# A two-layer recurrent decoder step: the last layer norm taken apart, and the variance products of the others moved

## The chip, the cores and the metric

The kernel runs on one core of a Trainium2 chip. A core has a matrix engine (TensorE, PE in the profile), a vector engine (VectorE, DVE), an engine for activation functions (ScalarE, ACT), a general one (GpSimd, POOL) and a synchronisation engine (SyncE, SP), each with its own instruction queue, and 16 DMA engines. The metric is device time in microseconds. The time before is 1552.72 us, the median of three runs (1552.39 to 1553.37).

## The reference

One step of a decoder trunk with two layers (width 1024), over a prompt of 512 tokens and 8 samples of 4 tokens. Layer 0 mixes by mLSTM and gated linear attention, layer 1 by a Mamba-2 state space mixer (SSD); each is followed by a squared-ReLU MLP. After each of the four blocks stands a layer norm over the features:

```python
def _layernorm(x, g, b):
    xf = x.astype(jnp.float32)
    mu = xf.mean(-1, keepdims=True)
    var = jnp.square(xf - mu).mean(-1, keepdims=True)
    y = (xf - mu) * lax.rsqrt(var + LN_EPS) * g.astype(jnp.float32) + b.astype(jnp.float32)
    return y.astype(x.dtype)

def _mlp(x, w1, w2):
    return jnp.square(jax.nn.relu(x @ w1)) @ w2
...
x = LN(DN_ALPHA * x + mix(x))
x = LN(DN_ALPHA * x + mlp(x))
```

## The kernel before

**Layout.** The 544 tokens are two halves of 272 columns (`TH`). Activations lie feature-major: a tile is 128 features by 272 tokens, and `KT` = 8 tiles make the width. `xf[hf]` holds the eight float32 tiles of a half, `xh` and `xl` their high and low parts for the matrix engine. A float32 product is made of three fast ones, high by high, high by low, low by high. `dense` (L359) issues them for one output tile and half: 24 for eight tiles of contraction, into one of three PSUM buffers (`psd`), and then the eviction, VectorE's add of `psd` to `xf` (L390, L392). I call one product of `dense` a dense product.

**Weights.** SyncE loads a weight block into `wraw` (three buffers), ScalarE makes its high part `whi` (L166), VectorE the low part `wlo` (L167), 1024 columns at a time.

**Order.** TensorE's order is written out by hand. Beside the dense products run lanes, Python generators that issue other TensorE work: `tick()` advances them ahead of each dense product, and a generator that yields the number N is left alone for N dense products. The table `W` holds these numbers. The order on VectorE, ScalarE, GpSimd and SyncE is made by a scheduler from a timeline that it simulates for the whole program. So a change of one place also moves instructions of these four engines elsewhere.

**The norms.** The last `phase` of a block runs tile 0 of both halves, then tiles 1 to 7 of half 0, then 1 to 7 of half 1 (`TAIL` = 7; behind the first mixer it is all eight). `residual` evicts a tile and adds it to the half's running sum `lns`, on GpSimd for tiles 1 to 6 (L396, L398) and on VectorE for tile 7. After a half's last tile `layernorm` is launched as a lane:

- the mean product L411, a matmul with a matrix of ones, which sums over the 128 features of `lns`
- four operations of two tiles each that take the mean off (VectorE, L416), and their squares `lnq` (ScalarE, L417)
- four adds that bring the eight squares down to one tile (GpSimd L419, VectorE L420 to L422)
- after `v0` = 60 (half 0) or `v1` = 55 (half 1) dense products the variance product L426
- logarithm and exponential for the inverse root (ScalarE, L428, L429)
- eight scalings (VectorE, L432), and the high, low and full parts for the next block (L439 to L441).

There are four norms: behind the first mixer, behind the first MLP (`mlp`), behind the SSD mixer (`ssd_out`) and behind the second MLP, which is the last. The last writes its tiles to the output (L434, and a transfer per pair). For its half 1 nothing dense is left: it leaves tile 7 out of the running sum (`short`), adds it by a second mean product (L413), and takes all eight squares as eight variance products (L426) in place of the adds.

**The SSD mixer.** In its first group, around 750 us, ScalarE copies convolution inputs `ci` from PSUM (L1351, L1354, L1356), issues small transfers from its queue, among them `dec` (L1317) and `decs` (L1319, two, decay factors of the samples broadcast to 64 partitions) and `ec` (L1408), and takes the activation `Cf` (L1369). VectorE makes the columns `scols` and `ncs` (L1335, L1336). The diff doesn't touch these lines.

## Time and profile before

| what | value |
|---|---|
| median of three runs | 1552.72 us |
| the profiled execution's own time | 1552.4 us |
| its span | 1550.5 us |
| TensorE busy | 1490.8 us, 96% |
| VectorE busy | 1086.5 us, 70% |
| ScalarE busy | 794.7 us, 51% |
| GpSimd busy | 307.3 us, 20% |
| granted TensorE clock, mean | 0.99 |

The busy time of a matmul is modelled and overlaps with that of the next, so 96% does not mean that TensorE is at its best; its waits are what counts. The span is the time between the first and the last profiled instruction. A row of the waits names who waits and for whom, then the wait in all, how often, and the longest. A row of the timeline has the start, the duration of one instruction or the busy time of several (x8), the engine, the line, the operation, output and input by the program's names, and in square brackets the engine's idle time ahead of it with what ended it. The chain has start, duration, engine and line of the work that ended last, in order of time. In a row of the windows stand the window, its length, then busy time and instructions of an engine.

### The profile page before, as it was taken

What the parts mean: (1) busy time and instruction counts of PE and PEld (TensorE: products, weight loads), DVE (VectorE), ACT (ScalarE), POOL (GpSimd) and SP (SyncE); (2) the same over time, 40 slices, a digit from 0 to 9 for tenths busy, and PEclk for the clock granted to TensorE, in tenths of its full rate; (3) what the DMA queues carried; (4) which work ended last, traced back from release to release, by engine and by line L of the source; (5) the groups of instructions that cost most, each with busy time, mean ns of one, the idle gap of its engine ahead of it and who ended that gap; (6) DMA issues with size and microseconds to landing.
All of it is one profiled execution on the core that took longest, in us unless ns stands there. A gap on an engine that the chain in (4) does not pass through costs nothing.

```text
span 1550.5 us, 29292 instructions
## 1 busy us (share of the span) xinstructions
PE 1490.8 (96%) x11621; PEld 1436.3 (93%) x11621; DVE 1086.5 (70%) x2029; ACT 794.7 (51%) x1749; POOL 307.3 (20%) x369
## 2 busy tenths in 40 slices
PE   8899999999999999999899999999899999999997
PEld 7799988999999999999797789989899999999996
DVE  4963466686776677658799978667768767676644
ACT  5543455474444444537685766645238344344333
POOL 0420223310000000043253464533330000000011
PEclk9999999999999999999999999999999999999999
DMA  6221222513333233415547768364213333323221
GB/s 217 65 83 55 59 87 69 180 39 97 96 105 94 89 96 85 146 40 198 114 125 248 209 180 261 96 208 136 69 34 87 99 85 105 97 86 95 66 83 58
DMA packets 88400, 172.11 MB, mean 111 GB/s; under 512 B 15464, under 2 KB 41960, under 8 KB 88008
## 3 DMA queue, kind: packets, MB, share of 16 engines
q1 hardware_dynamic: 52296, 141.20, 29.2%
q10 hardware_dynamic: 33376, 18.42, 4.8%
q0 software_dynamic: 2592, 10.62, 1.7%
q8 instruction: 91, 1.49, 0.4%
q14 instruction: 45, 0.37, 0.1%
HBM read 153.48 MB, written 16.73 MB: 110 GB/s over the span
## 4 chain that ended last, share of the span: by engine, by line
PE 79%; DVE 7%; ACT 3%; DMA 2%; issue 2%; ACTq 1%; POOL 0%; DVEq 0%; SPq 0%; POOLq 0%
PE psd L359 53%; PE psd L449 16%; DVE wlo L167 1%; PE num L693 1%; ACT whi L166 1%; PE yp L1472 1%; DMA E<-d_cs 1%; PE it L1519 1%; PE sp L1450 1%; DVE xf L416 1%; DVE h0n L1532 1%; DVE xl L1586 1%; PE var L426 1%; PE ip L1447 1%; ACTq L1319 1%
## 5 line engine op out<-in xcount | busy, mean ns | idle before, releaser
L359 PE MATMUL psd<-xh,whi 128*128 128x272 f32 x1504 | 447.5, 298 | 7.4 <-ACT xh L283 6.0
L359 PE MATMUL psd<-xh,wlo 128*128 128x272 f32 x1504 | 443.6, 295 | 0.2 <-DVE wlo L167 0.2
L359 PE MATMUL psd<-xl,whi 128*128 128x272 f32 x1504 | 442.8, 294 | 0.3 <-DVE xl L284 0.3
L359 PEld LDWEIGHTS psd<-xh,whi 128*128 128x128 f32 x1504 | 287.0, 191 | 14.1 <-ACT xh L283 6.4
L359 PE MATMUL psd<-hh,whi 128*128 128x272 f32 x1024 | 296.6, 290 | 3.6 <-DVE xf L392 2.5
L359 PE MATMUL psd<-hlo,whi 128*128 128x272 f32 x1024 | 295.4, 289 | 0.2
L359 PE MATMUL psd<-hh,wlo 128*128 128x272 f32 x1024 | 295.4, 288 | 0.0
L359 PEld LDWEIGHTS psd<-xl,whi 128*128 128x128 f32 x1504 | 287.0, 191 | 6.6 <-issue 4.0
L359 PEld LDWEIGHTS psd<-xh,wlo 128*128 128x128 f32 x1504 | 286.7, 191 | 4.5 <-issue 3.0
L166 ACT CAST whi<-wraw 128x1024 fp32r<-128x1024 f32 (+2 forms) x173 | 174.4, 1011 | 160.6 <-PE psd L359 138.2
L167 DVE TENSOR_TENSOR wlo<-wraw,whi 128x1024 fp32r<-128x1024 f32 (+2 forms) x173 | 210.2, 1217 | 65.8 <-ACT whi L166 65.1
L359 PEld LDWEIGHTS psd<-hh,whi 128*128 128x128 f32 x1024 | 192.8, 188 | 5.8 <-DVE xf L392 4.4
L359 PEld LDWEIGHTS psd<-hlo,whi 128*128 128x128 f32 x1024 | 192.8, 188 | 0.7 <-DVE hlo L284 0.6
L359 PEld LDWEIGHTS psd<-hh,wlo 128*128 128x128 f32 x1024 | 192.7, 188 | 0.1
L392 DVE TENSOR_TENSOR xf<-xf,psd 128x272 f32<-128x272 f32 x208 | 88.3, 433 | 92.2 <-PE psd L359 91.4
L396 POOL TENSOR_TENSOR lns<-xf 128x272 f32<-128x272 f32 x8 | 9.1, 1138 | 684.1 <-DVE xf L392 678.8
L449 PE MATMUL psd<-xh,whi 128*128 128x272 f32 x416 | 120.2, 289 | 0.9 <-DVE xf L392 0.9
L449 PE MATMUL psd<-xh,wlo 128*128 128x272 f32 x416 | 119.9, 288 | 0.0
L449 PE MATMUL psd<-xl,whi 128*128 128x272 f32 x416 | 119.6, 288 | 0.0
L202 ACT CAST whi<-wsum 128x1024 fp32r<-128x1024 f32 x52 | 54.3, 1044 | 121.4 <-PE psd L449 72.1
L202 ACT CAST whi<-wraw 128x1024 fp32r<-128x1024 f32 (+1 forms) x52 | 43.4, 835 | 96.6 <-PE psd L359 85.3
L203 DVE TENSOR_TENSOR wlo<-wsum,whi 128x1024 fp32r<-128x1024 f32 x52 | 63.7, 1224 | 23.2 <-ACT whi L202 23.2
(448 smaller groups left out, 2962.4 us busy)
## 6 DMA issues: line engine op xcount, KB each, us to landing
wraw<-mlp_w SPq DMA_DIRECT2D x80, 512.0 KB, 3.6
wraw<-ssd_in SPq DMA_DIRECT2D x40, 512.0 KB, 4.3
wraw<-mlp_w SPq DMA_DIRECT2D x64, 256.0 KB, 3.1
wraw<-ab_in SPq DMA_DIRECT2D x24, 512.0 KB, 3.7
h<-h SPq DMA_DIRECT2D x32, 256.0 KB, 4.6
h0n<-h0n SPq DMA_DIRECT2D x16, 512.0 KB, 5.0
E<-d_cs ACTq DMA_DIRECT2D x16, 512.0 KB, 5.1
s_h<-h0n POOLq DMA_DIRECT2D x16, 512.0 KB, 4.0
```

Source lines behind the costliest of these rows:

```text
L166: nc.scalar.copy(hi[:, r], w[:, r])
L167: nc.vector.tensor_tensor(lo[:, r], w[:, r], hi[:, r].bitcast(F32), ALU.subtract)
L202: self.cut[0] = nc.scalar.copy(hi, x).ins
L203: self.cut[1] = nc.vector.tensor_tensor(lo, x, hi.bitcast(F32), ALU.subtract).ins
L359: last[0] = TE.matmul(ps[:, :TH], wt[:, k, :], rt, start=i == 0, stop=i == n - 1).ins
L392: V.tensor_tensor(x, x, ps, ALU.add)
L416: V.scalar_tensor_tensor(x[:, k:k + 2], mu[:, None, :n].broadcast_to([P, 2, n]), -1.0 / D, x[:, k:k + 2], ALU.mult, ALU.add)
L426: TE.matmul(var[:, :n], ones, q[:, k], start=k == 0, stop=k == KT - 1 or not short)
L449: last[0] = TE.matmul(ps, wt[:, k], bt[:, k], start=first and n == 0, stop=n == 11, skip_group_check=not first).ins
L693: TE.matmul(num[i], sT[:, i] if j == i else sT[:, (4, 7, 9)[j] + i - j - 1], vt[key][:, j, h, :w], start=j == 0, stop=j == i)
L1319: S.dma_start(out=decs[64 * e:64 * e + 64], in_=d_dec[None, e::2, 4:].broadcast_to([64, 16, NB]))
L1447: TE.matmul(ip[:, j * P:(j + 1) * P], hT[:, j * P:(j + 1) * P], Cf[:, tk], start=True, stop=True)
```

## The change

The variance product of `layernorm` moves from 60 to 76 dense products behind the start of its wait in half 0, and from 55 to 62 in half 1. Half 1 of the last norm gets a function of its own, `last_layernorm`, launched at the eviction of tile 5:

- after `f0` = 10 dense products the mean product of the sum of six tiles (tiles 0 to 5); this mean m6 is taken off all eight tiles, the tiles that aren't finished included, and the first six are squared and added up
- after `f1` = 30 more the variance product of these squares; then, for tile 6 and for tile 7 when each is evicted, a mean product and a variance product of that tile
- the mean that is left over is that of tiles 6 and 7 (the first six now sum to nought), and the variance is the mean of squares less its square (L480, L481)
- logarithm and exponential, the left-over mean taken off in four operations, and `normed`, the scalings and transfers as before.

`short` falls away. The diff:

```diff
-W = dict(..., l0=12, l1=12, v0=60, v1=55)
+W = dict(..., l0=12, l1=12, v0=76, v1=62, f0=10, f1=30)
...
-    def residual(first, ln=None, short=False):
+    def residual(first, ln=None, last_norm=None):
...
             if ln is not None:
-                if m == 1:
+                if hf and last_norm is not None and m >= KT - 2:
+                    ready.add(("last", m))
+                elif m == 1:
                     sums[hf] = ln.tile([P, TH], F32, tag="lns", name="lns", bufs=2)
                     G.tensor_tensor(sums[hf], xf[hf][:, 0], x, ALU.add)
-                elif m > 1 and not (short and hf and m == KT - 1):
+                elif m > 1:
                     (V if m == KT - 1 else G).tensor_tensor(sums[hf], sums[hf], x, ALU.add)
+                if hf and last_norm is not None and m == KT - 3:
+                    launch(last_norm(), "last")
...
-        short = out is not None and hf == 1
-        TE.matmul(mu[:, :n], ones, sums[hf], start=True, stop=not short)
-        if short:
-            TE.matmul(mu[:, :n], ones, x[:, KT - 1], start=False, stop=True)
+        TE.matmul(mu[:, :n], ones, sums[hf], start=True, stop=True)
...
-        for k in range(KT if short else 1):
-            TE.matmul(var[:, :n], ones, q[:, k], start=k == 0, stop=k == KT - 1 or not short)
+        TE.matmul(var[:, :n], ones, q[:, 0], start=True, stop=True)
...
+        if out is not None:
+            normed(x, g, b, rs, out[hf])
+            return
...
+    def last_layernorm(i, pool, out):
+        g, b = lnp[:, 16 * i:16 * i + 8], lnp[:, 16 * i + 8:16 * i + 16]
+        n, x = TH, xf[1]
+
+        def less(mu, k, f):
+            V.scalar_tensor_tensor(x[:, k:k + 2], mu[:, None, :n].broadcast_to([P, 2, n]), f, x[:, k:k + 2], ALU.mult, ALU.add)
+        yield W["f0"]
+        mu = pm("mu")
+        TE.matmul(mu[:, :n], ones, sums[1], start=True, stop=True)
+        q = pool.tile([P, KT, n], F32, tag="lnq", name="lnq", bufs=1)
+        less(mu, 6, -1.0 / (6 * P))
+        for k in (0, 2, 4):
+            less(mu, k, -1.0 / (6 * P))
+            S.activation(q[:, k:k + 2], x[:, k:k + 2], AF.Square)
+        V.tensor_tensor(q[:, 0:2], q[:, 0:2], q[:, 2:4], ALU.add)
+        V.tensor_tensor(q[:, 0:2], q[:, 0:2], q[:, 4:6], ALU.add)
+        V.tensor_tensor(q[:, 0], q[:, 0], q[:, 1], ALU.add)
+        yield W["f1"]
+        yield from need(("last", KT - 2))
+        mu, var = pm("mu"), pm("var")
+        TE.matmul(var[:, :n], ones, q[:, 0], start=True, stop=False)
+        for k in (6, 7):
+            yield from need(("last", k))
+            TE.matmul(mu[:, :n], ones, x[:, k], start=k == 6, stop=k == 7)
+            S.activation(q[:, k], x[:, k], AF.Square)
+            TE.matmul(var[:, :n], ones, q[:, k], start=False, stop=k == 7)
+        ms, v = q[:, 0], q[:, 1]
+        with tc.high_priority():
+            S.activation(ms, mu[:, :n], AF.Square, scale=1.0 / D)
+            V.scalar_tensor_tensor(v, var[:, :n], 1.0 / D, ms, ALU.mult, ALU.subtract)
+        rs = pool.tile([P, n], F32, tag="lnr", name="lnr", bufs=2)
+        S.activation(rs, v, AF.Ln, bias=epsc)
+        S.activation(rs, rs, AF.Exp, scale=-0.5)
+        for k in range(0, KT, 2):
+            less(mu, k, -1.0 / D)
+        normed(x, g, b, rs, out[1])
...
-                phase(8, hrhs(m), n, residual(False, xp, out is not None), tail=TAIL,
-                      after=lambda hf: launch(layernorm(hf, 2 * l + 1, xp, out)))
+                end = None if out is None else lambda: last_layernorm(2 * l + 1, xp, out)
+                phase(8, hrhs(m), n, residual(False, xp, end), tail=TAIL,
+                      after=lambda hf: launch(layernorm(hf, 2 * l + 1, xp, out)) if end is None or hf == 0 else None)
```

Lines of the new program are numbered anew: the evictions are L391 and L393, the running sum L399 and L401, the norm's mean product L415, its subtraction L418, its variance product stays L426, scalings are L435 (L443 in `normed`), low parts L437, and the SSD lines stand 47 later (`decs` L1366, `Cf` L1416).

What stands in the engines' queues now is shown at three places. The first is the end of the program. On TensorE, before, the last dense products of tile 7 of half 1 and what follows them:

```order
L359 MATMUL psd<-hh,wlo 128x272
L411 MATMUL mu<-lns,ones 128x272
L413 MATMUL mu<-xf_12707,ones 128x272
L426 MATMUL var<-lnq,ones 128x272 x8
L1865 UNCONDITIONAL_BRANCH
```

Now the mean product of six tiles (L460) stands 31 dense products ahead of the first of these rows:

```order
L472 MATMUL var<-lnq,ones 128x272
L475 MATMUL mu<-xf_12707,ones 128x272
L477 MATMUL var<-lnq,ones 128x272
L359 MATMUL psd<-hh,wlo 128x272
L359 MATMUL psd<-hh,whi 128x272
L359 MATMUL psd<-hlo,whi 128x272
L359 MATMUL psd<-hh,wlo 128x272
L359 MATMUL psd<-hh,whi 128x272
L359 MATMUL psd<-hlo,whi 128x272
L359 MATMUL psd<-hh,wlo 128x272
L475 MATMUL mu<-xf_12707,ones 128x272
L477 MATMUL var<-lnq,ones 128x272
```

Seven dense products stand between the products of tile 6 and those of tile 7, and two small products behind the last dense one where ten stood before.

On VectorE at the same place, before, from the last add of half 0's squares on (`xf_12702` is half 0 of `xf`, `xf_12707` half 1):

```order
L422 TENSOR_TENSOR lnq<-lnq 128x272
L392 TENSOR_TENSOR xf_12707<-xf_12707,psd 128x272
L432 SCALAR_TENSOR_TENSOR xf_12702<-xf_12702,lnp,lnr 128x272 x8
L392 TENSOR_TENSOR xf_12707<-xf_12707,psd 128x272 x4
L416 SCALAR_TENSOR_TENSOR xf_12707<-mu,xf_12707 128x544 x4
L432 SCALAR_TENSOR_TENSOR xf_12707<-xf_12707,lnp,lnr 128x272 x8
```

And now, from half 0's scalings on:

```order
L443 SCALAR_TENSOR_TENSOR xf_12702<-xf_12702,lnp,lnr 128x272 x8
L393 TENSOR_TENSOR xf_12707<-xf_12707,psd 128x272
L457 SCALAR_TENSOR_TENSOR xf_12707<-mu,xf_12707 128x544 x4
L393 TENSOR_TENSOR xf_12707<-xf_12707,psd 128x272
L466 TENSOR_TENSOR lnq<-lnq 128x544
L467 TENSOR_TENSOR lnq<-lnq 128x544
L468 TENSOR_TENSOR lnq<-lnq 128x272
L393 TENSOR_TENSOR xf_12707<-xf_12707,psd 128x272
L457 SCALAR_TENSOR_TENSOR xf_12707<-mu,xf_12707 128x544
L481 SCALAR_TENSOR_TENSOR lnq<-var,lnq 128x272
L457 SCALAR_TENSOR_TENSOR xf_12707<-mu,xf_12707 128x544 x3
L443 SCALAR_TENSOR_TENSOR xf_12707<-xf_12707,lnp,lnr 128x272 x8
```

Three evictions of half 1 (tiles 5, 6 and 7) stand behind half 0's scalings, with the subtraction of m6 and the adds of squares between them; four stood there before, with nothing between.

The second place is the norm behind the SSD mixer, on VectorE, from half 0's scalings to half 1's subtraction. Before:

```order
L432 SCALAR_TENSOR_TENSOR xf_12702<-xf_12702,lnp,lnr 128x272 x8
L440 SCALAR_TENSOR_TENSOR xl_75<-xf_12702,lnp,xh_73 128x272 x2
L392 TENSOR_TENSOR xf_12707<-xf_12707,psd 128x272
L440 SCALAR_TENSOR_TENSOR xl_75<-xf_12702,lnp,xh_73 128x272 x6
L392 TENSOR_TENSOR xf_12707<-xf_12707,psd 128x272
L167 TENSOR_TENSOR wlo<-wraw,whi 128x1024
L392 TENSOR_TENSOR xf_12707<-xf_12707,psd 128x272
L167 TENSOR_TENSOR wlo<-wraw,whi 128x1024
L392 TENSOR_TENSOR xf_12707<-xf_12707,psd 128x272
L398 TENSOR_TENSOR lns<-lns,xf_12707 128x272
L167 TENSOR_TENSOR wlo<-wraw,whi 128x1024
L416 SCALAR_TENSOR_TENSOR xf_12707<-mu,xf_12707 128x544 x4
```

Now, from the low parts on:

```order
L437 SCALAR_TENSOR_TENSOR xl_75<-xf_12702,lnp,xh_73 128x272 x4
L393 TENSOR_TENSOR xf_12707<-xf_12707,psd 128x272
L437 SCALAR_TENSOR_TENSOR xl_75<-xf_12702,lnp,xh_73 128x272
L167 TENSOR_TENSOR wlo<-wraw,whi 128x1024
L437 SCALAR_TENSOR_TENSOR xl_75<-xf_12702,lnp,xh_73 128x272 x3
L393 TENSOR_TENSOR xf_12707<-xf_12707,psd 128x272
L167 TENSOR_TENSOR wlo<-wraw,whi 128x1024
L393 TENSOR_TENSOR xf_12707<-xf_12707,psd 128x272
L167 TENSOR_TENSOR wlo<-wraw,whi 128x1024
L401 TENSOR_TENSOR lns<-lns,xf_12707 128x272
L167 TENSOR_TENSOR wlo<-wraw,whi 128x1024
L418 SCALAR_TENSOR_TENSOR xf_12707<-mu,xf_12707 128x544 x4
```

Between half 0's scalings and the last add to `lns` there were two weight differences (L167), and there are three now.

The third place is ScalarE in the first group of the SSD mixer, around 750 us. Before:

```order
L166 CAST whi<-wraw 128x1024
L1408 DMA ec<-d_ecs 64x4x128
L1354 COPY ci<-psd 128x240
L1356 COPY ci<-psd 128x8x4
L1351 COPY ci<-psd 128x272
L1317 DMA dec<-d_dec 128x32x4
L1319 DMA decs<-d_dec 64x16x8 x2
L1369 ACTIVATE Cf<-acc 128x512
L1370 ACTIVATE Cf<-acc 128x32
```

Now:

```order
L1455 DMA ec<-d_ecs 64x4x128 x2
L1411 ACTIVATE acc<-ci,sprm 128x568
L1455 DMA ec<-d_ecs 64x4x128
L1450 DMA E_9382<-d_cs 32x8x32
L1364 DMA dec<-d_dec 128x32x4
L1398 COPY ci<-psd 128x272
L1366 DMA decs<-d_dec 64x16x8 x2
L1401 COPY ci<-psd 128x240
L166 CAST whi<-wraw 128x1024
L1403 COPY ci<-psd 128x8x4
L1416 ACTIVATE Cf<-acc 128x512
```

The transfers `dec` and `decs` stand behind more transfers than before (`ec`, `E`), and between `decs` and `Cf` there are now a copy, a weight cast and another copy.

More of the change, by code (lines that the diff above doesn't have):

```diff
@@ L33 @@
 HEADM = 6
-W = dict(dec=12, gates=400, sc=16, lev=12, v=8, kd=10, out=33, end=12, c0=15, u=11, s=16, ml=12, dt=238, sg=72, sx=14, sq=26, so=48, l0=12, l1=12, v0=60, v1=55)
+W = dict(dec=12, gates=400, sc=16, lev=12, v=8, kd=10, out=33, end=12, c0=15, u=11, s=16, ml=12, dt=238, sg=72, sx=14, sq=26, so=48, l0=12, l1=12, v0=76, v1=62, f0=10, f1=30)
 LEVELS = (64, 32, 16, 8, 4, 2, 1)
@@ L417, in layernorm @@
             S.activation(q[:, k:k + 2], x[:, k:k + 2], AF.Square)
-        if not short:
-            G.tensor_tensor(q[:, 0:2], q[:, 0:2], q[:, 2:4], ALU.add)
-            V.tensor_tensor(q[:, 4:6], q[:, 4:6], q[:, 6:8], ALU.add)
-            V.tensor_tensor(q[:, 0:2], q[:, 0:2], q[:, 4:6], ALU.add)
-            V.tensor_tensor(q[:, 0], q[:, 0], q[:, 1], ALU.add)
-            yield W["v1" if hf else "v0"]
+        G.tensor_tensor(q[:, 0:2], q[:, 0:2], q[:, 2:4], ALU.add)
+        V.tensor_tensor(q[:, 4:6], q[:, 4:6], q[:, 6:8], ALU.add)
+        V.tensor_tensor(q[:, 0:2], q[:, 0:2], q[:, 4:6], ALU.add)
+        V.tensor_tensor(q[:, 0], q[:, 0], q[:, 1], ALU.add)
+        yield W["v1" if hf else "v0"]
         var = pm("var")
-        for k in range(KT if short else 1):
-            TE.matmul(var[:, :n], ones, q[:, k], start=k == 0, stop=k == KT - 1 or not short)
+        TE.matmul(var[:, :n], ones, q[:, 0], start=True, stop=True)
         rs = pool.tile([P, n], F32, tag="lnr", name="lnr", bufs=2)
@@ L432, in layernorm @@
             V.scalar_tensor_tensor(xk, xk, gk, rs, ALU.mult, ALU.mult)
-            if out is not None:
-                S.activation(xk, xk, AF.Identity, bias=bk)
-                if k % 2 or k == KT - 2:
-                    k0 = k if k >= KT - 2 else k - 1
-                    nc.sync.dma_start(out=out[hf][:, k0:k + 1], in_=x[:, k0:k + 1])
-                continue
             S.activation(xh[hf][:, k], xk, AF.Identity, bias=bk)
@@ L441, in layernorm, with normed @@
             S.activation(xk, xk, AF.Identity, bias=bk)
+    def normed(x, g, b, rs, out):
+        for k in range(KT):
+            xk = x[:, k]
+            V.scalar_tensor_tensor(xk, xk, g[:, k:k + 1], rs, ALU.mult, ALU.mult)
+            S.activation(xk, xk, AF.Identity, bias=b[:, k:k + 1])
+            if k % 2 or k == KT - 2:
+                k0 = k if k >= KT - 2 else k - 1
+                nc.sync.dma_start(out=out[:, k0:k + 1], in_=x[:, k0:k + 1])
+    def last_layernorm(i, pool, out):
[12 more added lines that the diff above has]
+        V.tensor_tensor(q[:, 0:2], q[:, 0:2], q[:, 2:4], ALU.add)
+        V.tensor_tensor(q[:, 0:2], q[:, 0:2], q[:, 4:6], ALU.add)
+        V.tensor_tensor(q[:, 0], q[:, 0], q[:, 1], ALU.add)
+        yield W["f1"]
[17 more added lines that the diff above has]
+        normed(x, g, b, rs, out[1])
     def quarter(w, b, ps, first):
```

## The prediction

> **What bounds the kernel now.** I read the page first, then TensorE's waits, over the whole span and in the windows of the norms, then the chain at the end, then the timelines of the places that the change touches.
>
> ```profile
> span 1550.5 us, 29292 instructions
> ...
> DVE  4963466686776677658799978667768767676644
> ...
> PE 79%; DVE 7%; ACT 3%; DMA 2%; issue 2%; ACTq 1%; POOL 0%; DVEq 0%; SPq 0%; POOLq 0%
> ```
>
> TensorE carries 79% of the chain that ends last. So the time falls only where TensorE waits, and in the stretch behind its last product; work that only moves on another engine costs nothing until TensorE waits for it. VectorE's row has three slices of 38.8 us at 9 (the 21st to 23rd, 775 to 891 us, in the SSD mixer): there a delay on VectorE isn't made up. TensorE's waits that bear on the change:
>
> ```profile
> PE xt L1411 <- DVE ncs L1336: 6.4, 1, 6.4
> ...
> PE var L426 <- ACT lnq L417: 1.6, 1, 1.6
> ```
>
> In the windows 300 to 310, 676 to 690, 1145 to 1155 and 1164 to 1176 us the variance product's wait reads, in turn:
>
> ```profile
> PE var L426 <- DVE lnq L422: 1.5, 1, 1.5
> ...
> PE var L426 <- DVE lnq L422: 0.5, 1, 0.5
> ...
> PE var L426 <- DVE lnq L422: 1.6, 1, 1.6
> ...
> PE var L426 <- DVE lnq L422: 0.6, 1, 0.6
> ```
>
> The columns are the wait in all, how often, the longest. I call the three norms A (behind the first mixer), B (behind the first MLP) and C (behind the SSD mixer). Half 0 of A, B and C waits 1.5, 0.5 and 1.6 us, half 1 of C 0.6: **4.2 us** is all that moving the variance products can win. The 1.6 us of `ACT lnq` is in the end chain, which the new last norm replaces:
>
> ```profile
> 1535.54 0.45 DVE xf L392
> ...
> 1536.87 0.73 DVE xf L416
> 1537.63 0.67 ACT lnq L417
> 1538.34 3.95 PE var L426 x16
> 1542.31 0.49 ACT lnr L428
> ...
> 1543.29 0.51 DVE xf L432
> ```
>
> From the eviction of the last tile to the first scaling is 1543.29 - 1535.54 = 7.75 us, 3.95 of it the eight variance products, 0.49 each.
>
> **The change, part by part.** (1) *Variance products later.* How far one dense product moves another is read from a window at the end:
>
> ```profile
> 1524.00:1534.00 10.00, 10.00 (x82) 10.00 (x81) 1.00 0.31 113
> ```
>
> It counts 82 products, some two of which began before it: 10 / 80 = 0.125 us each. 16 products later is 2.0 us, more than the 1.6 of any half 0; 7 later is 0.88, more than the 0.6. So each of the four waits goes, and I ask at each what is late next. B: nothing (VectorE's slice there reads 5), -0.5. A: ScalarE's new order has a weight cast between the norm's logarithm and its exponential, and that cast waited for its weights:
>
> ```profile
> 310.69 1.05 ACT L166 CAST whi<-wraw 128x1024 fp32r<-128x1024 f32 x1 [1.88 <-DMA wraw<-mlp_w]
> ...
> 324.15 0.62 PE L411 MATMUL mu<-lns,ones 128*128 128x272 f32 x2
> ```
>
> The scalings of half 0 then start late, and the sums of half 1, due at the second row, with them. The cost lies between nothing, if the 12 us from the cast's end make it up, and the whole 1.88 + 1.05; I take 0.3, since those 12 us hold mostly VectorE work that can close up. A gives -1.2. C: VectorE has no gap between the scalings of half 0 and the mean product of half 1:
>
> ```profile
> 1156.29 3.08 DVE L440 SCALAR_TENSOR_TENSOR xl<-xf,lnp,xh 128x272 fp32r<-128x272 f32 x6
> 1159.64 1.21 DVE L167 TENSOR_TENSOR wlo<-wraw,whi 128x1024 fp32r<-128x1024 f32 x1
> 1163.25 0.44 DVE L398 TENSOR_TENSOR lns<-lns,xf 128x272 f32<-128x272 f32 x1
> ...
> 1164.01 0.62 PE L411 MATMUL mu<-lns,ones 128*128 128x272 f32 x2
> ```
>
> The new order puts three weight differences of 1.2 us ahead of the last sum (`lns`) instead of two. So the sum ends no earlier than before, though TensorE gets there 1.6 us sooner, and half 0's 1.6 is given back; half 1's 0.6 stays. Ends: 0 to -1.6 for half 0, and I take 0, because the extra row's 1.21 nearly fills it. **Sum: -1.2 - 0.5 - 0.6 = -2.3**, with ends -4.2 and 0.
>
> (2) *The end chain.* Behind the last eviction the new program needs the mean product (from 1535.54 to 1536.87 before: 1.33 us to the first subtraction), four subtractions, one variance operation of 272 columns and the first scaling. Their rows:
>
> ```profile
> 1514.86 0.62 PE L411 MATMUL mu<-lns,ones 128*128 128x272 f32 x2
> ...
> 1515.53 2.62 DVE L416 SCALAR_TENSOR_TENSOR xf<-mu,xf 128x544 f32<-128x544 f32 x4 [0.98 <-PE mu L411]
> 1516.34 2.49 ACT L417 ACTIVATE lnq<-xf 128x544 f32<-128x544 f32 x4 [23.98 <-DVE xf L416]
> ...
> 1520.39 0.72 DVE L421 TENSOR_TENSOR lnq<-lnq 128x544 f32<-128x544 f32 x1
> ...
> 1524.61 3.39 DVE L432 SCALAR_TENSOR_TENSOR xf<-xf,lnp,lnr 128x272 f32<-128x272 f32 x8 [1.13 <-ACT lnr L429]
> ```
>
> 1.33 + 2.62 + 0.42 (a scaling, 3.39 / 8, the nearest row to the variance operation) = 4.37. Logarithm and exponential (0.49 and 0.46) lie beside the last three subtractions, which cover them. So the first scaling is 7.75 - 4.37 = **3.4 us earlier after the eviction**. What follows it (eight scalings, ScalarE's bias, the transfer) is the same code.
>
> But the eviction itself comes later. Ahead of it are now four fp32 products that weren't (mean and variance of six tiles, mean and variance of the seventh): 4 x 0.49 = 2.0. And two new waits. The mean product L460 stands 38 dense products ahead of the last, so it is due 38 x 0.125 = 4.75 us before the old one:
>
> ```profile
> 1529.51 0.44 DVE L392 TENSOR_TENSOR xf<-xf,psd 128x272 f32<-128x272 f32 x1 [1.16 <-PE psd L359]
> ...
> 1530.10 0.77 POOL L398 TENSOR_TENSOR lns<-lns,xf 128x272 f32<-128x272 f32 x1 [0.83 <-DVE xf L392]
> ...
> 1535.34 0.62 PE L411 MATMUL mu<-lns,ones 128*128 128x272 f32 x2
> ```
>
> That is at 1530.6. It needs the sum of tile 5, whose eviction is the row of 1529.51. Half 0's scalings (3.39 us from 1524.61) are pushed 2.0 us back with their variance product, and in VectorE's order they stand ahead of tile 5's eviction: from 1526.6, or 1526.8 behind tile 4's eviction, to 1530.2, or 1530.7 if GpSimd's add of tile 4 holds one up. So tile 5 is evicted up to 1.2 us late; GpSimd's add starts 0.59 later and takes 0.77: 1531.6 to 1532.1, a wait of 1.0 to 1.5; I take 1.2. Next, the first variance product L472 stands 31 dense products behind, 0.49 + 31 x 0.125 = 4.4 us, and needs 0.67 (mean to subtraction), 2.62, the last square's 0.62, two adds of 0.72 and 0.44, which is 5.1, or 5.5 with an eviction in the way: a wait of 0.7 to 1.1, and I take 1.1, as an eviction does stand there. **Sum: 2.0 + 1.2 + 1.1 - 3.4 = +0.9**; without both waits it is -1.4, with both twice as long +3.2.
>
> The 0.5 is from a pair of rows at C. The first was shown: six operations in 3.08 us, 0.5 more than six of 0.42. The second ran beside them:
>
> ```profile
> 1156.51 0.91 POOL L398 TENSOR_TENSOR lns<-lns,xf 128x272 f32<-128x272 f32 x1 [5.24 <-issue]
> ```
>
> The Trainium skill, page "SBUF — State Buffer", section "Who interferes with whom", has a rule that speaks against this change here: VectorE and GpSimd share one port pair, an exclusive lock, and a VectorE instruction with two SBUF inputs contends with a GpSimd instruction that reads SBUF. These rows agree. By the rule the wait at L460 is 1.5, without it 1.0; the value taken lies between.
>
> (3) *The SSD mixer's first group.* The other engines' order is set by the scheduler's own simulated time, and it comes out differently there, though no line of it is edited. It holds TensorE's longest wait for VectorE, the 6.4 us at 765:
>
> ```profile
> 754.48 0.36 ACT L1354 COPY ci<-psd 128x240 f32<-128x240 f32 x1 [2.89 <-DVE acc L1366]
> ...
> 754.74 0.20 ACT L1356 COPY ci<-psd 128x32 f32<-128x32 f32 x1
> ...
> 755.05 8.13 ACTq L1319 DMA_DIRECT2D decs<-d_dec  x2
> 763.23 0.63 ACT L1369 ACTIVATE Cf<-acc 128x512 f32<-128x512 f32 x1 [8.01 <-issue]
> ...
> 764.60 0.42 DVE L1335 COPY scols<-rt 128x256 f32<-128x256 f32 x1
> ```
>
> ScalarE stands 8.13 us in issuing two transfers (`decs`), and `Cf`, the column copies and TensorE are behind it. In the new order three things that ran ahead of `decs`, or far from it, stand between `decs` and `Cf`: a copy of 0.36, a weight cast of 1.05 (row at 310.69) and a copy of 0.20: +1.6 if `decs` starts and blocks as before. It may start up to 2.9 us earlier (the 2.89 that ScalarE idled), or be blocked longer, since more transfers (`ec`, `E`) are issued ahead of it; half of 8.13 once more is +4, +5.5 with the 1.6. Ends: -6.4 (the wait gone) and +5.5; I take **+1.6**, the one part with rows of its own.
>
> The Trainium skill, page "DMA: Bandwidth & Descriptors", section "Issuing engines are not separate DMA queues", says that the time an engine's sequencer spends starting a DMA is usually small beside the DMA itself. The row of 8.13 us disagrees. By the rule this order would cost nothing and the sum would be 1.6 lower.
>
> **The sum.** -2.3 + 0.9 + 1.6 = +0.2 on the profiled execution's own 1552.4 (1.9 more than its span): **1552.6 us**, no change. The median of the runs, 1552.72, is 0.3 above that execution, within their spread. About 0.2%, 3.1 us, is what a measurement of this kernel can tell from no change.
>
> **The rivals.**
> *Faster.* The weight differences at C fall where VectorE would idle and the sums of the last half are in time: -4.2 and -1.4, with the SSD mixer as it was: 1546.8 us; with (1) as taken, 1548.7. For it: the waits are there in the trace, and every bound of (2) is within 1.5 us of no wait. Against it: VectorE's order at C. Chance 0.25.
> *Slower.* One mechanism, the `decs` issue: if it blocks ScalarE over 2.9 us longer (from where -2.3 + 0.9 + 1.6 + 2.9 = +3.1), TensorE's wait at 765 grows, and VectorE's full slices don't give it back: with +5.5 it is -2.3 + 0.9 + 5.5 = +4.1, 1556.5 us. For it: ScalarE's queue row and the transfers now ahead of it. Against it: the 2.89 of idle time. Chance 0.20.
> *The SSD order costs nothing:* -2.3 + 0.9, 1551.0 us. Chance 0.10. This is the time that the skill's rule on issuing gives.
> *The change doesn't bite:* the variance products wait on, because what makes `lnq` is pushed back by the same evictions: +0.9 + 1.6, 1554.9 us. Against it: 2.0 covers 1.6. Chance 0.07.
> *The forecast* 0.38.
>
> Same: 0.38 + 0.10 + 0.07 = 0.55; faster 0.25; slower 0.20. The range leaves out half of each outer case: 1548 to 1556.5.
>
> **What would show it.** (1): the rows `PE var` for L422's successor are gone; at C the mean product of half 1 is as late behind half 0's variance product as the lost 1.6. (2): from last eviction to first scaling 4.4 us; waits for `lns` and `lnq` of some 1 us each, 5 us before the end. (3): the row `PE xt` near 765 reads about 8. It is wrong if TensorE's waits change in places that I haven't looked at, as in other groups of the SSD mixer, where the order changes little.

## The result, and the profile after

The changed kernel takes 1556.89 us (median of 13 runs, 1554.82 to 1560.26), the kernel before 1551.94 us (13 runs, 1547.12 to 1554.68): 1.0038 times as long, with a 95% interval of 1.0029 to 1.0047. It is slower by 5.0 us in the medians, 5.9 by the ratio. The forecast was 1552.6 us in a range of 1548 to 1556.5.

The page of the changed kernel, its span and the chain's shares by engine:

```profile
span 1555.7 us, 29290 instructions
...
PE 39%; DVE 6%; ACT 3%; issue 2%; DMA 2%; POOL 1%; ACTq 1%; POOLq 0%; DVEq 0%
```

The chain that this page follows back from the end breaks off at 741 us, so its shares add up to about half of the span and can't be set beside the 79% before. TensorE's waits in it (in all, how often, the longest):

```profile
PE xt L1458 <- DVE ncs L1383: 8.5, 1, 8.5
...
PE mu L415 <- DVE lns L401: 3.9, 3, 2.7
...
PE psd L359 <- ACT ci L1403: 1.7, 1, 1.7
...
PE mu L460 <- POOL lns L401: 1.4, 1, 1.4
...
PE var L472 <- DVE lnq L468: 1.1, 1, 1.1
```

The variance products at A, B and C wait no more, 4.2 us before. In their place the **mean products** of half 1 wait for `lns`: 3.9 us in three waits of 0.6, 0.6 and 2.7, which weren't there. The wait of `xt` in the SSD mixer grew from 6.4 to 8.5. The two waits of the new last norm are there as forecast.

Waits alone don't add up to a span, so I matched TensorE's instructions of the two traces in order and took the difference of their starts. One pair of rows, before and after, shows it:

```profile
765.36 0.66 PE L1411 MATMUL xt<-scon,Y 128*128 128x128 f32 x2 [6.39 <-DVE ncs L1336]
```

```profile
767.39 0.45 PE L1458 MATMUL xt<-scon,Y 128*128 128x128 f32 x1 [8.52 <-DVE ncs L1383]
```

There the changed kernel is 2.0 us behind. A part's cost is the difference behind it less that ahead of it, here with bounds at 290, 400, 712, 766, 1130, 1200 and 1515 us of the trace before, and the end of the span. All 17 traces (one of each kernel) are in the table, against the trace before, in us; the experiments follow below. "Ratio" is the timed one, to the kernel before.

| kernel | up to A | A | B | SSD, first group | SSD, rest | C | MLP | tail | ratio (95%) |
|---|---|---|---|---|---|---|---|---|---|
| the changed kernel | -0.3 | -0.5 | 0.3 | **2.5** | 0.4 | **1.6** | -0.4 | **1.6** | 1.0038 (1.0029 to 1.0047) |
| e1_vmove | -1.6 | -0.4 | 0.3 | 2.8 | -0.5 | 1.8 | -0.4 | 0.0 | 1.0030 (1.0017 to 1.0044) |
| e2_lastonly | -0.3 | 0.0 | 0.2 | -0.2 | -0.5 | 0.0 | -0.2 | 0.5 | 1.0011 (0.9997 to 1.0025) |
| e3_C | 2.6 | 0.0 | -0.1 | -0.3 | -0.8 | 0.2 | 0.0 | 0.5 | 1.0021 (1.0011 to 1.0031) |
| e4_AB | -0.1 | -0.6 | 0.1 | 2.7 | 0.3 | 0.0 | -0.3 | 0.4 | 1.0029 (1.0018 to 1.0041) |
| e5_v0 | 2.4 | -0.4 | 0.2 | 0.2 | 2.1 | 1.8 | -0.3 | 1.6 | 1.0016 (1.0002 to 1.0029) |
| e6_v1 | -0.8 | 0.0 | -0.1 | 2.8 | 0.0 | -0.8 | -0.5 | 0.4 | 1.0012 (0.9999 to 1.0026) |
| e7_tail | 0.7 | 0.0 | 0.1 | 0.0 | -3.1 | 0.0 | -0.2 | -0.8 | 0.9998 (0.9982 to 1.0013) |
| e8_decs | -2.0 | -0.5 | 0.1 | -1.8 | -0.1 | 0.2 | -0.4 | 1.7 | 1.0010 (0.9994 to 1.0027) |
| e9_best | -0.6 | -1.5 | -0.4 | 1.6 | -0.6 | 0.0 | -0.3 | -0.7 | 0.9980 (0.9972 to 0.9989) |
| e10_l1 | 5.4 | -0.5 | 0.0 | 2.9 | -2.9 | -2.4 | -0.4 | 1.6 | 1.0018 (1.0008 to 1.0029) |
| e11_v0site | -0.7 | -1.5 | -0.3 | 0.4 | 0.4 | 0.0 | -0.4 | -0.7 | 0.9989 (0.9974 to 1.0004) |
| e12_decs0 | 1.1 | 0.0 | 0.0 | 0.3 | -2.9 | 0.0 | -0.3 | 0.1 | 1.0001 (0.9990 to 1.0012) |
| e13_dec0 | 0.1 | 0.0 | -0.1 | -4.1 | 2.9 | 0.0 | -0.4 | 2.0 | 1.0008 (0.9994 to 1.0022) |
| e14_dec1 | 0.1 | -0.5 | 0.0 | -4.2 | 2.7 | 0.2 | -0.4 | 1.7 | 1.0018 (1.0005 to 1.0031) |
| e15_decbest | 0.6 | -1.5 | -0.4 | -4.3 | 2.8 | 0.0 | -0.4 | -0.7 | 0.9978 (0.9963 to 0.9992) |
| e16_all | -0.8 | -1.5 | -0.4 | -4.3 | 6.7 | -2.4 | -0.3 | -0.7 | 0.9955 (0.9938 to 0.9973) |

The columns "up to A" and "SSD, rest" differ between kernels in which nothing was edited there: they are what one execution differs from another, up to 5 and 7 us. The "MLP" column is the same in nearly all, so it is the trace before that was long there. The other columns repeat to a few tenths of a microsecond wherever the same code runs, with two exceptions that are explained below (C and one tail). On them the verdicts rest, with the timed ratios behind them.

### The profile page after: what moved, and what is told of

Its sections match the earlier page's. It is cut to its first block, busy times and chain, and to the rows that moved or that the text cites. A ratio compares the mean times of both kernels' runs of the same rounds, so it can differ in the third digit from the quotient of the medians.

```text
span 1555.7 us, 29290 instructions
## 1 busy us (share of the span) xinstructions
PE 1490.7 (96%) x11613; PEld 1436.4 (92%) x11613; DVE 1088.7 (70%) x2037; ACT 795.5 (51%) x1751; POOL 306.3 (20%) x368
## 4 chain that ended last, share of the span: by engine, by line
PE 39%; DVE 6%; ACT 3%; issue 2%; DMA 2%; POOL 1%; ACTq 1%; POOLq 0%; DVEq 0%
PE psd L359 26%; PE psd L495 8%; DMA E<-d_cs 1%; DVE wlo L167 1%; ACT E L1479 1%; PE it L1566 1%; PE yp L1519 1%; DVE acc L1413 1%; DVE h0n L1579 1%; DVE xl L1633 1%; PE sps L1573 1%; ACT whi L166 1%; PE sp L1497 1%; DVE xf L393 0%; ACTq L1366 0%
## 5 line engine op out<-in xcount | busy, mean ns | idle before, releaser
L167 DVE TENSOR_TENSOR wlo<-wraw,whi 128x1024 fp32r<-128x1024 f32 (+2 forms) x173 | 208.5, 1207 | 73.0 <-ACT whi L166 69.5
L393 DVE TENSOR_TENSOR xf<-xf,psd 128x272 f32<-128x272 f32 x208 | 88.1, 432 | 94.2 <-PE psd L359 93.7
L399 POOL TENSOR_TENSOR lns<-xf 128x272 f32<-128x272 f32 x8 | 9.1, 1139 | 684.3 <-DVE xf L393 678.9
```

Of the source, the lines that this page charges most:

```text
L167: nc.vector.tensor_tensor(lo[:, r], w[:, r], hi[:, r].bitcast(F32), ALU.subtract)
L393: V.tensor_tensor(x, x, ps, ALU.add)
```

## The experiments: which part costs

Four kernels take the change apart. The first is the kernel before with the numbers alone, the second the changed kernel without them:

```diff
e1_vmove (on the kernel before)
-v0=60, v1=55
+v0=76, v1=62
e2_lastonly (on the changed kernel)
-v0=76, v1=62
+v0=60, v1=55
```

> The kernel before with the two numbers alone moved (v0 76, v1 62), its last norm as it was. Theory (the waits of the variance products were only traded: half 0's scalings and low parts, pushed back by 16 products, now hold up the sum of half 1, and ScalarE's and VectorE's new order in the SSD mixer's first group adds to that): slower by 3 to 5 us, ratio 1.002 to 1.003; no wait of L426 at the three inner norms, but waits of the mean product for lns of some 0.6, 0.6 and 2.7 us, and the wait of xt near 765 some 2 us longer than before. Rival (the loss is the new last norm's, moved variance products win what their waits were): faster by 2 to 4 us, ratio 0.998. Rival (SSD differences are chance from run to run): ratio 1.000.

> The changed kernel with v0 60 and v1 55 as before, so only the new last norm is left of the change; SSD mixer's queues are as before. Theory: half 0's scalings are 2 us earlier than in the changed kernel, so the wait for lns at L460 (1.4 there) is under 0.5; the wait for lnq at L472 stays 1.1; 2.0 of added products + 0.4 + 1.1 - 3.4 = 0.1 us: ratio 0.999 to 1.001. Rival (the loss is in the last norm): slower by 3 us or more, 1.002.

The other two move the products at one place alone, with the new last norm in:

```diff
-        yield W["v1" if hf else "v0"]
+        v0, v1 = (W["v0"], W["v1"]) if i in (2,) else (60, 55)      # e3_C; (0, 1) for e4_AB
+        yield v1 if hf else v0
```

> As the one before, but with the variance products moved (76, 62) at the norm behind the SSD mixer alone; the SSD mixer's queues are as before. Theory: the 1.6 and 0.6 us of waits there go, and a wait for lns of some 2.7 us comes at half 1's mean product: 0.5 to 1.6 us slower than with the new last norm alone. Rival (the moved product is worth its wait): 2 us faster than that.

> As the kernel with the new last norm alone, but with the variance products moved (76, 62) at the first two norms alone; this brings the SSD mixer's other order of ScalarE and VectorE. Theory: norms +0.1 (2.0 of waits gone, as much come back as waits for lns and for the scalings), SSD +2.8: 2 to 3.5 us slower than with the new last norm alone. Rival (the SSD difference is chance): within 0.7 us of it, with the wait of xt near 765 at 6 to 7 us.

Measured: 1.0030, 1.0011, 1.0021 and 1.0029. The loss is in the moved products: they alone make the kernel 4.7 us slower, and the rival that they win what their waits were falls. The last norm alone is not told from no change by the time; its tail is 0.5 us longer in the trace. Both together give 1.0041 against 1.0038 measured. The waits of e1_vmove for `lns` and at `xt`:

```profile
PE xt L1411 <- DVE ncs L1336: 8.8, 1, 8.8
...
PE mu L411 <- DVE lns L398: 3.9, 3, 2.7
```

They come with the numbers alone. Two more kernels tell which of the two numbers brings the SSD mixer's new order: in the first the order of ScalarE and VectorE there is nearly that of before, in the second that of the changed kernel.

```diff
-v0=76, v1=62
+v0=76, v1=55      # e5_v0
+v0=60, v1=62      # e6_v1
```

> The changed kernel with v1 back at 55, so that of the moved variance products only half 0's are left. The SSD mixer's queues are then as before the change. Theory (the SSD mixer's loss comes with v1 alone; half 0's moved products trade their waits for waits for lns): no stall of some 1.9 us at 735, the wait of xt near 765 at 6 to 6.5 us, waits of the mean product for lns of 0.6, 0.6 and 2.7 us; against the new last norm alone between 0 and 1.5 us slower, so ratio 1.001 to 1.002 to the kernel before. Rival (half 0's moved products cost most): 1.003 or more.

> The changed kernel with v0 back at 60, so that only half 1's variance products are moved, by 7, which could win the one wait of 0.6 us. The SSD mixer's queues are those of the changed kernel. Theory: stall of 1.9 us at 735, xt waits 8.5 us, the waits of half 0's variance products (1.5, 0.5, 1.6) are back and those for lns gone; 2 us slower than the new last norm alone, ratio 1.002 to 1.003 to the kernel before. Rival (SSD difference is chance or is made up later): as the new last norm alone, 1.001.

The traces answer as the theory says: first group of SSD 0.2 against 2.8, C 1.8 against -0.8. The times don't settle the split: to e2_lastonly's 1.0011, v0 alone adds 0.0005, v1 alone 0.0001 and both together 0.0027, with intervals of 0.0013 to either side. The time of e6_v1 is even the one that its rival names (1.001), not the 1.002 to 1.003 of its theory. The 2.5 to 2.9 us of the first group stand in all five traces in which v1 is 62 ahead of the SSD mixer and no transfer was moved, and in none of the five with 55 there; how much of it lasts to the end is taken up with the runs on `dec` below.

**Why C gets worse.** VectorE behind the SSD mixer in the changed kernel, from half 0's scalings to half 1's sum, and the scalings before:

```profile
1154.59 3.90 DVE L435 SCALAR_TENSOR_TENSOR xf<-xf,lnp,lnr 128x272 f32<-128x272 f32 x8
...
1161.96 1.84 DVE L437 SCALAR_TENSOR_TENSOR xl<-xf,lnp,xh 128x272 fp32r<-128x272 f32 x3
...
1164.06 1.21 DVE L167 TENSOR_TENSOR wlo<-wraw,whi 128x1024 fp32r<-128x1024 f32 x1
...
1165.55 1.43 DVE L167 TENSOR_TENSOR wlo<-wraw,whi 128x1024 fp32r<-128x1024 f32 x1
1166.90 0.43 DVE L401 TENSOR_TENSOR lns<-lns,xf 128x272 f32<-128x272 f32 x1
```

```profile
1151.81 3.39 DVE L432 SCALAR_TENSOR_TENSOR xf<-xf,lnp,lnr 128x272 f32<-128x272 f32 x8 [1.46 <-ACT lnr L429]
```

The changed kernel is 2.4 us behind when it reaches C. Its scalings begin 2.8 us later than before, so 0.4 by the product itself: 2.0 less the 1.6 that it waits no more. Three weight differences follow, the last two of them shown, and the sum ends at 1167.33, 3.6 us later than before, so 1.2 by C itself. TensorE, which got there sooner, stands for it from 1164.71. Behind that wait something else appears. The windows of the changed kernel and of e3_C, which has the same wait of 2.7 us at 1166.41 (columns: window, length, TensorE's busy time and count, its weight loads, VectorE, ScalarE, GpSimd, granted clock, DMA share, GB/s):

```profile
1168.00:1170.00 2.00, 2.00 (x9) 1.88 (x8) 1.77 (x4) 0.49 (x1) 0.00 (x0) 0.50 0.80 214
```

```profile
1168.00:1170.00 2.00, 2.00 (x19) 2.00 (x18) 2.00 (x4) 1.78 (x5) 0.21 (x1) 1.00 0.74 232
```

In the one the granted clock is 0.50 and 9 products run in 2 us, in the other it is 1.00 and 19 run. The same wait is followed by half clock in three of the six traces that have it (the changed kernel, e1_vmove, e5_v0) and not in the other three (e3_C, e8_decs, e14_dec1): those are the two values of column C, 1.6 to 1.8 and 0.2.

Where the wait lies decides it. In each trace all changes of the granted clock stand on one grid of 3.413 us: the half clock at C lasts one such step in each of the three, and in the changed kernel the next change follows 378.9 us after it, 111 steps. This is the step of each trace's grid that holds most of the wait, in us (where the clock doesn't change at C, the grid is counted back from its next change):

| kernel | step | TensorE busy in it | granted clock in the next step |
|---|---|---|---|
| the changed kernel | 1163.63 to 1167.04 | 1.08 | 0.50 |
| e1_vmove | 1163.26 to 1166.67 | 1.16 | 0.50 |
| e5_v0 | 1167.40 to 1170.81 | 1.53 | 0.50 |
| e3_C | 1164.68 to 1168.09 | 1.68 | 1.00 |
| e14_dec1 | 1161.44 to 1164.85 | 1.68 | 1.00 |
| e8_decs | 1156.17 to 1159.58 | 1.86 | 1.00 |

The same wait halves the clock here where it leaves TensorE 1.53 us of work or less in one step, and not where the grid cuts it so that 1.68 or more is left. The Trainium skill, page "TensorE: Matmul & The Clock Gate", section "Part 1: The HAM clock gate (the "warmup" mystery)", has a gate that grants full or half clock by how busy TensorE was in a free-running window of some 3.4 us. The trace agrees in the two values and in the window (3.41 us). The same section lets the clock fall behind an idle window; here one with 1.53 us of work was enough.

If the mean product is what stands too early, it can be moved:

```diff
e10_l1 (on the changed kernel)
-        yield W["l1" if hf else "l0"]
+        yield 34 if hf and i == 2 else W["l1" if hf else "l0"]
```

> The changed kernel with half 1's mean product behind the SSD mixer 22 dense products later (34 in place of 12), and the rest of that half's norm with it; other places as changed. Theory (TensorE stands 2.7 us before this product because VectorE makes the sum late, and after it the granted clock is at half for up to 3.5 us more): the 2.7 us wait goes, no half clock at 1165 to 1172; 2.7 to 4.2 us faster than the changed kernel, ratio 1.001 to 1.002 to the kernel before. Rival (the wait only moves again, to the start of the next MLP, which needs half 1's parts): a wait of the first dense products of half 1 for xh or xl of 2 us or more, and 1.003 to 1.004 as before.

Measured 1.0018, 3.1 us less than the changed kernel. TensorE has no wait for `lns` or `lnq` from 1140 to 1182, and no wait for `xh` or `xl` follows. The same window in it, now with the mean product among the dense ones:

```profile
1168.00:1170.00 2.00, 2.00 (x16) 1.85 (x16) 2.00 (x4) 1.85 (x4) 0.30 (x1) 1.00 0.49 192
```

The granted clock is 1.00. Column C turns from +1.6 to -2.4: the 2.2 us of waits that the kernel before has there are won at last, when all three products of the chain move. Half 1's variance product alone (e6_v1) wins 0.8 there.

**Why A wins less.** ScalarE in the changed kernel behind A's variance product:

```profile
307.85 0.49 ACT L428 ACTIVATE lnr<-var,epsc 128x272 f32<-128x272 f32 x1 [1.66 <-PE var L426]
309.92 1.05 ACT L166 CAST whi<-wraw 128x1024 fp32r<-128x1024 f32 x1 [1.58 <-DMA wraw<-mlp_w]
310.87 0.42 ACT L429 ACTIVATE lnr<-lnr 128x272 f32<-128x272 f32 x1
```

And before:

```profile
307.86 0.49 ACT L428 ACTIVATE lnr<-var,epsc 128x272 f32<-128x272 f32 x1 [1.41 <-PE var L426]
308.38 0.43 ACT L429 ACTIVATE lnr<-lnr 128x272 f32<-128x272 f32 x1
```

The cast does stand between logarithm and exponential and waits for its weights: the exponential comes at 310.87, 2.5 us later than before, and the sum of half 1 is late for 0.6 us of TensorE. The other half of the question is whether products moved less far would do:

```diff
e11_v0site (on e7_tail, below)
-        yield W["v1" if hf else "v0"]
+        yield W["v1"] if hf else (72, 64, 60, 60)[i]
```

> The kernel of the shortened last norm (v0 60, v1 55), with half 0's variance product moved only as far as its wait was long, and only where the sum of half 1 had time to spare: 72 behind the first mixer, 64 behind the first MLP, 60 behind the SSD mixer. Theory (up to its wait the product's own time doesn't move, so nothing behind it is pushed back; beyond it, everything is): the waits for lnq of 1.5 and 0.5 are under 0.2, none over 0.2 for lns; 1.5 to 2 us faster than the shortened last norm alone, ratio 0.998 to 0.999 to the kernel before. Rival (waits are traded whole): waits for lns of 1 us or more at these two sites, ratio 1.000.

Measured 0.9989 (0.9998 for e7_tail). No wait for `lnq` or `lns` is left at A and B, and the columns read -1.5 and -0.3 instead of -0.5 and +0.3. As long as the product is moved no further than it waited, its own time stays and nothing behind it is pushed. At A this run doesn't part the shorter move from ScalarE's order: the cast no longer stands between logarithm and exponential in it (307.13 and 307.65). At B no cast stood there in either kernel. The difference of the two ratios is within their intervals; the columns carry this.

## The experiments: the tail and the SSD mixer's first group

**The tail.** From the last eviction to the first scaling, the chain of the changed kernel:

```profile
1543.96 0.45 DVE xf L393
...
1548.60 0.42 DVE xf L443
```

4.64 us, where it was 7.75 and 4.37 was forecast. Ahead of it, VectorE and then GpSimd and TensorE at L460:

```profile
1530.48 3.90 DVE L443 SCALAR_TENSOR_TENSOR xf<-xf,lnp,lnr 128x272 f32<-128x272 f32 x8
1534.31 0.42 DVE L393 TENSOR_TENSOR xf<-xf,psd 128x272 f32<-128x272 f32 x1
```

```profile
1530.70 0.90 POOL L401 TENSOR_TENSOR lns<-lns,xf 128x272 f32<-128x272 f32 x1 [2.69 <-DVE xf L393]
1534.87 0.76 POOL L401 TENSOR_TENSOR lns<-lns,xf 128x272 f32<-128x272 f32 x1 [3.27 <-DVE xf L393]
```

Half 0's scalings take 3.90 instead of 3.39 beside GpSimd's add of 0.90, hold up tile 5's eviction, and L460 waits 1.4 us. In e2_lastonly, with half 0's product at 60, that wait is 0.2 and the tail 0.5 instead of 1.6. The next kernel takes away more of what the last norm puts ahead of the last product:

```diff
e7_tail (on e2_lastonly)
-f0=10, f1=30
+f0=10, f1=26, f2=7
-                    (V if m == KT - 1 else G).tensor_tensor(sums[hf], sums[hf], x, ALU.add)
+                    (V if m == KT - 1 or (hf and last_norm is not None and m == KT - 3) else G).tensor_tensor(...)
+        TE.matmul(mu[:, :n], ones, x[:, 6], start=True, stop=False)
+        S.activation(q[:, 6], x[:, 6], AF.Square)
+        V.tensor_tensor(q[:, 0], q[:, 0], q[:, 6], ALU.add)
+        yield W["f2"]
         TE.matmul(var[:, :n], ones, q[:, 0], start=True, stop=False)
-        for k in (6, 7):
-            ...
+        yield from need(("last", 7))
+        TE.matmul(mu[:, :n], ones, x[:, 7], start=False, stop=True)
+        S.activation(q[:, 7], x[:, 7], AF.Square)
+        TE.matmul(var[:, :n], ones, q[:, 7], start=False, stop=True)
```

> v0 60 and v1 55, and the last norm changed: tile 5 is added to the sum by VectorE in place of GpSimd, tile 6's square is added to the other squares, so that there are two variance products in place of three, and the first of them comes ten dense products later. Theory (what the new last norm costs are four added products and the waits at L460 and for lnq): one product less (0.5), no wait for lns (0.2) and none for lnq (1.1): 1.5 to 2 us faster than the new last norm alone, ratio 0.999 to 1.000 to the kernel before, the stretch from the last eviction to the first scaling unchanged. Rival (the loss is behind the last eviction): no gain.

Measured 0.9998, 2 us less than e2_lastonly; the tail column goes from 0.5 to -0.8, and a wait of 0.7 for `lnq` remains. So by the tail column the new last norm is worth 0.8 us when its sums and products are nearly in time, and costs 1.6 when they aren't; by the time alone, 0.9998 is no change.

**The first group.** VectorE and ScalarE there in the changed kernel:

```profile
762.13 1.23 DVE L167 TENSOR_TENSOR wlo<-wraw,whi 128x1024 fp32r<-128x1024 f32 x1 [6.50 <-ACT whi L166]
763.27 0.69 DVE L1418 SCALAR_TENSOR_TENSOR Cf<-Cf,acc 128x512 f32<-128x512 f32 x1
...
763.99 0.68 DVE L1418 SCALAR_TENSOR_TENSOR Y<-Y,acc 128x512 f32<-128x512 f32 x1
...
765.06 1.65 DVE L1413 SCALAR_TENSOR_TENSOR acc<-ci,sprm,acc 128x568 f32<-128x568 f32 x2 [0.29 <-ACT acc L1411]
766.63 0.42 DVE L1382 COPY scols<-rt 128x256 f32<-128x256 f32 x1
```

```profile
753.66 7.09 ACTq L1366 DMA_DIRECT2D decs<-d_dec  x2
...
762.07 0.64 ACT L1416 ACTIVATE Cf<-acc 128x512 f32<-128x512 f32 x1
```

ScalarE is free of `decs` at 760.75, 2.4 us sooner than before, and `Cf` comes at 762.07, 1.2 us sooner. But on VectorE a weight difference (1.23), `Y` and two steps of `acc` (1.65) now stand ahead of the columns `scols` and `ncs`, which before followed `Cf` at once. So the columns come 2.0 us later, and not for the reason that I gave. This is read from the queues of one trace; no run sets VectorE's order alone. Is ScalarE's block behind it all the same?

```diff
e8_decs (on the changed kernel), e12_decs0 (on the kernel before)
-                S.dma_start(out=decs[64 * e:64 * e + 64], ...)
+                G.dma_start(out=decs[64 * e:64 * e + 64], ...)
```

> The changed kernel with the two decs transfers issued from GpSimd's queue in place of ScalarE's. Theory (ScalarE stands 7 to 8 us in issuing them, and Cf, the columns ncs and TensorE's xt are behind it): ScalarE has no gap of more than 2 us there, the wait of xt near 765 falls from 8.5 us to under 4; 4 to 6 us faster than the changed kernel, ratio 0.998 to 1.001 to the kernel before. Rival (the transfers ahead fill the DMA engines, and E or the weights come late anyway): xt still waits 6 us or more and the time stays at 1.003 or above.

> The kernel before with decs issued from GpSimd's queue, nothing else. Theory (ScalarE's 8 us in issuing decs make the 6.4 us wait of xt): xt waits under 3 us, 2 to 5 us faster, ratio 0.997 to 0.999. Rival (VectorE sets that stretch, the win is given back by 830 us): xt waits under 3 us, ratio 0.9995 to 1.000.

In e8_decs `xt` waits 2.2 us, as its theory has it, and the ratio is 1.0010, at the edge of its range; but a transfer of ScalarE still stands, 4.73 us. So the edit went into a kernel of all that had won so far:

> All that won so far together: the last norm with two variance products and VectorE's add of tile 5, decs from GpSimd's queue, v1 55, and half 0's variance products moved only as far as each site's wait (72 behind the first mixer, 64 behind the first MLP, 60 elsewhere). Theory: tail -0.9, site moves -1.9, decs -2 to -4, together 5 to 7 us faster than the kernel before, ratio 0.9955 to 0.997. Rival (VectorE sets the SSD mixer's length, so that the win at xt is given back): 0.998 to 0.999.

That kernel is e11_v0site with the edit of e8_decs. It measured 0.9980, short of its theory and not told from e11_v0site's 0.9989, and `xt` waits 8.1 us in it, so not for its rival's reason either. And e12_decs0 gave 1.0001 with `xt` waiting 6.8 us. Its ScalarE queue shows why:

```profile
755.57 0.40 ACTq L1317 DMA_DIRECT2D dec<-d_dec  x1
...
756.08 7.42 ACTq L1408 DMA_DIRECT2D ec<-d_ecs  x1
```

With `decs` gone it is `ec` that stands 7.42 us: whatever is issued next behind `dec` stands (8.80 for `ec` in e9_best, 4.73 for `E` in e8_decs, which has more of ScalarE's work ahead of it by its order). `dec` is 64 KB that the program spreads as 128 x 32 pieces of four numbers; that the small pieces are the reason is a guess that no run tests. So the next edit moves `dec` itself, on the kernel before, on the changed one, and on e11_v0site:

```diff
-            S.dma_start(out=dec, ...)
+            G.dma_start(out=dec, ...)
```

> The kernel before with the one transfer dec issued from GpSimd's queue, and decs left with ScalarE. Theory (it is dec, with its many small packets, that fills ScalarE's queue; whatever transfer is issued next there stands 7 to 9 us, decs or ec): no row of ScalarE's queue over 2 us there, xt waits under 3 us. If that wait counts in the end, 2 to 5 us faster, ratio 0.997 to 0.999. Rival (VectorE's full slices give it back): xt waits under 3 us, ratio 0.9995 to 1.000. Rival (the next transfer stands wherever dec is issued, as all share the DMA engines): a row of 5 us or more remains.

> The changed kernel with dec issued from GpSimd's queue. Theory: the wait of xt falls from 8.5 us to under 3; if that wait and its growth count in the end, 3 to 6 us faster than the changed kernel, ratio 1.000 to 1.002 to the kernel before, and equal to the kernel before with the same edit within what the norms and the tail cost (0.002). Rival (given back): 1.0025 or more.

> The shortened last norm, half 0's products moved only as far as their waits (72, 64, 60), and dec from GpSimd's queue. Theory: the 0.9989 of that kernel less the win at xt, 2 to 5 us: ratio 0.9955 to 0.9975. Rival (given back): 0.9985 to 0.9995.

In e13_dec0 `dec` takes GpSimd 1.73 us to issue, no transfer of ScalarE stands over 3.3 us (under 2 was expected), and the wait is

```profile
PE xt L1411 <- DVE ncs L1336: 2.9, 1, 2.9
```

against 6.4. Against the kernels that they were made from, the first group is 4.1, 6.7 and 4.7 us shorter in the three traces. But 2.9, 2.3 and 2.4 of it come back in the rest of the SSD mixer, where TensorE now waits for other things (2.2 us for `E` in e15_decbest, 1.5 in e13_dec0, 1.7 for `xw` in e14_dec1). The times say 1.0008, 1.0018 (from 1.0038) and 0.9978 (from 0.9989): the first interval holds no change, and the mean of the three is 0.0008 less than without the edit, about 1.2 us, with intervals of 0.0014 to either side of each. So of the 5.2 us that the edit wins there on the mean, the times keep a quarter and the traces half; what a microsecond at `xt` is worth in the end isn't settled. Whether the 2.5 that the changed kernel lost there count whole is not settled: the column behind them doesn't show them given back (0.4, -0.5, 0.3, 0.0, -2.9), but it is as wide as that in kernels without the loss.

The last run puts the site moves at C on top:

```diff
e16_all (on e15_decbest)
-        yield W["v1"] if hf else (72, 64, 60, 60)[i]
+        yield (62 if i == 2 else W["v1"]) if hf else (72, 64, 76, 60)[i]
-        yield W["l1" if hf else "l0"]
+        yield 34 if hf and i == 2 else W["l1" if hf else "l0"]
```

> The kernel of the run before (shortened last norm, products moved by 72 and 64 at the first two sites, dec from GpSimd's queue), and behind the SSD mixer the three numbers together: half 0's variance product 76, half 1's mean product 34, half 1's variance product 62. Theory (at that site the mean product is held to VectorE's sum, so the products must be moved together): no wait of 0.5 us or more for lnq or lns at 1140 to 1180, no half clock there, 2.4 us faster than the run before, ratio 0.9955 to 0.997. Rival (the next MLP then waits for half 1's parts): a wait of that size for xh or xl, ratio 0.9978 as before.

1545.42 us (median of 6), ratio 0.9955 (0.9938 to 0.9973): faster than both kernels, by the ratio 7 us faster than the one before. C reads -2.4, with no wait left there. The ratio lies at the end of its range. The 0.0023 to e15_decbest is 3.6 us, more than C's 2.4; the intervals cover the difference.

## Why the prediction was wrong

The three terms were forecast to sum to +0.2 us; in the trace they sum to +5.5.

**Moved variance products, forecast -2.3, measured +1.4** (-0.5, +0.3 and +1.6). The failing step is "each of the four waits goes, and I ask at each what is late next": I took it that 16 products (2.0 us) cover a wait and looked only at whether the cover was long enough. What it was too long by (0.5 at A, 1.5 at B, 0.4 at C) goes into half 0's scalings, and these stand on VectorE ahead of half 1's sum. At B I named nothing that was late; it was the sum, 0.6 us, and the pushed scalings met an add of GpSimd and took 3.90 us in place of 3.39. At A the place was right (the cast between logarithm and exponential) and its size wrong: 0.3 taken, 1.0 found, since the exponential was 2.5 us late and the 12 us behind it did not make that up. Of this 1.0, 0.6 is the wait for the sum; the rest isn't placed. At C I let the sum end as before. It ended 1.2 us later, so that the wait for it is 2.7 in place of the 1.6 that I gave back, which takes half 1's 0.6 with it; and I didn't see that a wait of 2.7 us may cost 1.5 more at half clock.

**The SSD mixer's first group, forecast +1.6, measured +2.5 to 2.9.** The step that failed is "if `decs` starts and blocks as before". The copy, the cast and the copy do stand behind it, 1.3 us from 760.79 to `Cf` at 762.07, but `decs` ended 2.4 us sooner, so `Cf` was not late. What stood in the way, by the trace, was VectorE's order behind `Cf`, which I did not set against that of before. That the price had the right sign was luck. (VectorE's row has a fourth slice at 9, the second, that I did not count; nothing rests on it.) The rival "slower" named 1556.5 us, close to what came, but by a longer block of ScalarE, which was shorter.

**The tail, forecast +0.9, measured +1.6.** Mechanism and places were right: 1.4 at L460 (1.2 taken), 1.1 at L472 (1.1), 0.5 lost to GpSimd's add (0.51 found), 3.1 saved behind the eviction (3.4). Only sizes were off.

All three terms erred to the same side, and the range took its bounds from a single trace, when runs of the kernel before spread over 7.6 us.

## What to carry to other kernels

A wait is won by moving what waits no further than the wait is long; each step beyond pushes everything that hangs on it, unless that is moved too, and the next wait is found by following the moved result through the other engines' queues, not by checking that the move covers the wait. Where one of a chain's products is held by another engine, move the chain together, or not at all. Where a scheduler sets the other queues, read the whole stretch of each queue that changed, VectorE's too, before putting a price on it.

## What the runs showed that I had not expected

A wait of TensorE of 2.7 us at C is followed by one 3.41 us step at half clock, 1.5 us lost, or by none, as the clock's grid cuts it. The tail of the kernel before is open to it too: in e13_dec0, whose last norm is that of before, the chain's eight variance products took

```profile
1536.84 5.63 PE var L426 x16
```

instead of 3.95 us. TensorE was busy for 1.76 us in the step ahead of them; in the trace before, the grid parts the same waits into two steps with 1.98 and 1.95. So no single number parts the cases: 1.68 kept the full clock at C. And a transfer of 64 KB in pieces of 16 bytes is issued in 0.4 us, while the next one on the same queue, whichever it is, holds its engine 4.7 to 8.8 us.
